# Three quarters of the MLP's second product as block multiplications with seven products each, on one Trainium2 core

## The chip, the core and the metric

The kernel runs on one core of one Trainium2 chip. The metric is the device time of one execution in microseconds (us). Before the change it is 3232.65 us, the median of 3 runs (3231.36 to 3234.63).

## What is computed

The reference is one inference step of a decoder with two trunk layers, run for 1024 prompt positions and 8 sample positions together (T = 1032 columns), model width D = 1024. Each layer is a mixer, a cross-attention into a memory, and an MLP with squared ReLU and hidden width 4096. Cut to what matters here:

```python
for l in range(DEPTH):                                  # DEPTH = 2
    x = x + mix                                         # pooling + RWKV-7 in layer 0, gated MLP in layer 1
    x = x + cross_attn(rmsnorm(x, norm_xa_g[l]), ...)
    x = x + sq_relu_mlp(rmsnorm(x, norm_ffn_g[l]), w_ff_up[l], w_ff_down[l])

def sq_relu_mlp(h, w_up, w_down):
    return jnp.square(jax.nn.relu(h @ w_up)) @ w_down
```

The change is in the product with `w_ff_down`: 4096 rows (32 K tiles of 128) by 1024 columns, times the hidden activations (4096 by 1032).

## The kernel before

All activations lie transposed, in tiles of 128 partitions by T columns. X is 8 such tiles, hidden is 32. A factor in fp32 is split into two fp32r parts: ScalarE copies the high part (line 194), and VectorE or GpSimd subtracts it from the source to get the low part (line 195). Three matmuls (high by high, high by low, low by high) then stand for one product. SBUF for tiles of T columns is a list of 42 slots that `get` takes from the front and `put` gives back at the end (lines 142 to 150); a load into a slot waits for the slot's last reader.

The MLP is `ffn` (line 1619).

**The first product** (line 1664) already goes through `strassen` (line 405). K and T are halved and the output rows go in pairs, so that a block of two output tiles by two halves of T takes seven half-size products instead of eight. A product is 24 matmuls of 258 columns: two quarters of T, four K tiles, three matmuls each (lines 426 to 428). For the left factors, `Left.make` (line 381) loads two weight units per pair (tag wraw, two buffers), forms up to four sums on VectorE and splits seven half-units into the tags whi and wlo (two buffers each). The right factors (`ops`, seven times four tiles) are made once. `collect` (line 437) takes the results out of PSUM and adds them up: ScalarE copies the first three, VectorE adds the rest, GpSimd adds twice (lines 452 and 456). `store` (line 1626) scales, squares and writes each half of a hidden tile to DRAM (hdn).

**The second product** (lines 1669 to 1704) is done in K blocks of 4, 8, 8, 8 and 4 tiles. The hidden tiles of a block are loaded from hdn and split (`hidden`, line 1633) while the block before it is computed. A block of 4 runs through `down` (line 1585), in the last layer the last one through `last` (line 1602). A block of 8 loops over the 8 output tiles: one weight unit, three groups of columns (384, 384, 264), 24 matmuls each, and VectorE adds the group from PSUM to X (line 1697). So a block of 8 has 192 matmuls each of three column groups, 576 in all.

A scheduler of the tile layer sets the order on each queue when the kernel is built; each engine and SyncE's DMA queue then work strictly in that order.

Of the kernel before, what the change touches and what calls it, by code (L numbers as in the profile page):

```python
# [74 lines left out]
SKIP = (0, 2)  # L75
STAY = 4
# [49 lines left out]
def hybrid_step(ctx: ExitStack, tc: tile.TileContext, I, O):  # L126
# [243 lines left out]
    class Left:  # L370


        def __init__(self, units):
            self.u, self.n, self.done = units, 0, deque()
# [6 lines left out]
        def make(self):  # L381
# [16 lines left out]
            split((a1, t, b1, t, a2, a2, b2)[j], w[:, 0:512], w[:, 512:1024])  # L398
# [970 lines left out]
    hdn = dr.tile([2, NFF, 128, T], F32, name="hdn")  # L1369

# [231 lines left out]
    def last(units, hid, nx):  # L1602

        wus = [(get(F32R), get(F32R)) for _ in units]
        for src, (hi, lo) in zip(units, wus):
            raw = sb.tile([128, 1024], F32, tag="wraw", bufs=2, name=nm("wr"))
            sy.dma_start(out=raw, in_=src)
            split(raw, hi[:, 0:1024], lo[:, 0:1024])
        nx.lag = LAG
        for g, (g0, g1) in enumerate(GR):  # L1610
            for m in range(KT):
                wh, wl = [t[:, (m % 2) * 512 : (m % 2) * 512 + 512] for t in wus[m // 2]]
# [6 lines left out]
    def ffn(l, nx, nname, then=None):  # L1619
# [23 lines left out]

        cur, w0, n = [], [], NFF // 2 * 7

        def fill(i):
# [8 lines left out]
            if j == 0:  # L1655
                raw = get()
                w0.extend(hpair())
                sy.dma_start(out=raw[:, 0:1024], in_=I[f"wd{l}"][0])
                split(raw[:, 0:1024], w0[0][:, 0:1024], w0[1][:, 0:1024])
                put(raw)  # L1660
# [3 lines left out]
        strassen(Left([I[f"wu{l}"][m] for m in range(NFF)]), nx.ops, lambda *a: collect(st, *a, store), fill=fill)  # L1664
# [4 lines left out]
        sizes = [4, 8, 8, 8, 4]  # L1669
        starts = [sum(sizes[:i]) for i in range(len(sizes))]  # L1670
        n2 = None
        for i, (k0, n) in enumerate(zip(starts, sizes)):
            nxt = []
            ahead = deque(range(starts[i + 1], starts[i + 1] + sizes[i + 1]) if i + 1 < len(sizes) else ())
            units = I[f"wd{l}"][k0 : k0 + n]
            if i == len(sizes) - 1:
                n2 = Next(None) if then else NextS(nname, xd[2])
                n2.lag = max(n2.lag, LAG)
                if then:
                    n2.then = lambda g: then(n2, g)  # L1680
                    last(units, cur, n2)
                    continue

            def more_hidden(k=1):
                for _ in range(min(k, len(ahead))):
                    nxt.append(hidden(ahead.popleft()))
# [354 lines left out]
```

## Time and profile before

| | |
|---|---|
| median of 3 runs | 3232.65 us |
| the profiled execution | 3233.54 us, span 3231.8 us |
| TensorE busy | 3138.2 us (97%), 22974 matmuls |
| VectorE, ScalarE, GpSimd busy | 59%, 36%, 20% |
| granted TensorE clock, mean | 0.986 |
| DMA | 416.07 MB, mean 129 GB/s |
| second product, blocks of 8 K tiles, layer 0 | about 1336 to 1609 us of the span |
| the same, layer 1 | about 2899 to 3170 us |

Matmul records overlap, so the length of one is not what it costs: the distance from one start to the next is. The same holds, less so, for VectorE, whose records overlap by 0.08 us where it has no wait. A row of the timeline gives start, length, engine, line, operation, output from input, shape and count, and in brackets the idle time before it with what ended it. The page names tiles without their numbers.

### The profile page before, as it was taken

What the parts mean: (1) busy time and instruction counts of PE and PEld (TensorE: products, weight loads), DVE (VectorE), ACT (ScalarE), POOL (GpSimd) and SP (SyncE); (2) the same over time, 40 slices, a digit from 0 to 9 for tenths busy, and PEclk for the clock granted to TensorE, in tenths of its full rate; (3) what the DMA queues carried; (4) which work ended last, traced back from release to release, by engine and by line L of the source; (5) the groups of instructions that cost most, each with busy time, mean ns of one, the idle gap of its engine ahead of it and who ended that gap; (6) DMA issues with size and microseconds to landing.
All of it is one profiled execution on the core that took longest, in us unless ns stands there. A gap on an engine that the chain in (4) does not pass through costs nothing.

```text
span 3231.8 us, 56258 instructions
## 1 busy us (share of the span) xinstructions
PE 3138.2 (97%) x22974; PEld 3015.0 (93%) x22974; DVE 1907.2 (59%) x3271; ACT 1162.7 (36%) x2218; POOL 651.2 (20%) x582
## 2 busy tenths in 40 slices
PE   8999799999999999999999999999999999999998
PEld 7988678898799999999999989899989999999998
DVE  4688644645457666532287897846445766662334
ACT  5223243434354444311163444224334544430111
POOL 5223334320031111000043351213002211100003
PEclk9999899999999999999999999999999999999999
DMA  3345677633423335432123354524342233461221
GB/s 120 119 144 188 125 244 230 223 108 116 159 92 102 106 118 181 159 104 67 48 91 126 112 200 154 171 72 138 118 165 99 87 106 112 131 233 54 91 72 66
DMA packets 188177, 416.07 MB, mean 129 GB/s; under 512 B 44301, under 2 KB 69261, under 8 KB 187918
## 3 DMA queue, kind: packets, MB, share of 16 engines
q1 hardware_dynamic: 168078, 392.01, 36.4%
q10 hardware_dynamic: 19840, 20.45, 2.3%
q8 instruction: 181, 2.97, 0.4%
q14 instruction: 78, 0.64, 0.1%
HBM read 297.23 MB, written 115.16 MB: 128 GB/s over the span
## 4 chain that ended last, share of the span: by engine, by line
PE 78%; DVE 10%; DMA 6%; ACT 2%; issue 2%; POOL 1%; SPq 0%; ACTq 0%; DVEq 0%; POOLq 0%
PE ps L225 15%; PE ps L226 15%; PE ps L227 15%; PE ps L428 8%; PE ps L426 8%; PE ps L427 8%; DVE s L195 1%; DVE wp L195 1%; DVE s L480 1%; PE ps L1469 1%; DMA wr<-in_w_in_c 1%; PE ps L1497 1%; PE ps L1825 1%; DMA wr<-in_wv 1%; DVE s L198 0%
## 5 line engine op out<-in xcount | busy, mean ns | idle before, releaser
L225 PE MATMUL ps<-s,wh 128*128 128x384 f32 (+2 forms) x3242 | 1046.4, 323 | 15.3 <-ACT wh L194 14.1
L227 PE MATMUL ps<-s,wl 128*128 128x384 f32 (+2 forms) x3242 | 1037.1, 320 | 2.7 <-DVE wl L195 2.7
L226 PE MATMUL ps<-s,wh 128*128 128x384 f32 (+2 forms) x3242 | 1038.2, 320 | 0.0
L426 PE MATMUL ps<-s,wp 128*128 128x258 f32 x2688 | 766.1, 285 | 3.6 <-DVE s L480 2.1
L428 PE MATMUL ps<-s,wp 128*128 128x258 f32 x2688 | 764.9, 285 | 4.2 <-DVE wp L195 4.2
L427 PE MATMUL ps<-s,wp 128*128 128x258 f32 x2688 | 762.6, 284 | 0.0
L225 PEld LDWEIGHTS ps<-s,wh 128*128 128x128 f32 x3242 | 612.5, 189 | 26.4 <-ACT wh L194 15.0
L227 PEld LDWEIGHTS ps<-s,wl 128*128 128x128 f32 x3242 | 611.5, 189 | 9.2 <-DVE wl L195 4.1
L226 PEld LDWEIGHTS ps<-s,wh 128*128 128x128 f32 x3242 | 612.3, 189 | 7.5 <-issue 6.0
L428 PEld LDWEIGHTS ps<-s,wp 128*128 128x128 f32 x2688 | 512.0, 191 | 6.5 <-DVE wp L195 6.2
L426 PEld LDWEIGHTS ps<-s,wp 128*128 128x128 f32 x2688 | 511.9, 190 | 6.0 <-issue 3.1
L427 PEld LDWEIGHTS ps<-s,wp 128*128 128x128 f32 x2688 | 512.9, 191 | 0.0
L265 POOL TENSOR_TENSOR s<-s,m 128x384 f32<-128x384 f32 (+1 forms) x147 | 164.0, 1124 | 1295.7 <-ACT m L264 1294.7
L194 ACT CAST wh<-wr 128x1024 fp32r<-128x1024 f32 x162 | 169.8, 1049 | 655.2 <-PE ps L226 598.3
L195 DVE TENSOR_TENSOR wp<-wr,wp 128x512 fp32r<-128x512 f32 x240 | 226.6, 944 | 177.6 <-ACT wp L194 176.5
L1697 DVE TENSOR_TENSOR s<-ps,s 128x384 f32<-128x384 f32 x144 | 74.3, 516 | 338.7 <-PE ps L227 338.7
L195 DVE TENSOR_TENSOR wl<-wr,wh 128x1024 fp32r<-128x1024 f32 x149 | 185.4, 1245 | 79.9 <-ACT wh L194 77.4
L194 ACT CAST wp<-wr 128x512 fp32r<-128x512 f32 x240 | 149.2, 622 | 148.5 <-PE ps L428 68.2
L195 DVE TENSOR_TENSOR s<-s,s 128x516 fp32r<-128x516 f32 (+4 forms) x168 | 158.0, 954 | 48.5 <-ACT s L194 47.6
L194 ACT CAST s<-s 128x516 fp32r<-128x516 f32 (+4 forms) x168 | 129.0, 788 | 87.0 <-DMA s<-hdn 43.2
L452 POOL TENSOR_TENSOR s<-s,s 128x516 f32<-128x516 f32 x40 | 59.2, 1480 | 490.7 <-ACT s L451 459.0
L1630 ACT ACTIVATE s<-s 128x516 f32<-128x516 f32 x128 | 81.3, 635 | 152.2 <-DVE s L478 152.2
(322 smaller groups left out, 4003.5 us busy)
## 6 DMA issues: line engine op xcount, KB each, us to landing
hdn<-s SPq DMA_DIRECT2D x128, 258.0 KB, 2.0
s<-hdn SPq DMA_DIRECT2D x64, 516.0 KB, 5.7
wr<-in_wu SPq DMA_DIRECT2D x64, 512.0 KB, 3.7
wr<-in_wd SPq DMA_DIRECT2D x62, 512.0 KB, 3.6
s<-in_kc SPq DMA_DIRECT2D x64, 256.0 KB, 3.9
s<-in_vc SPq DMA_DIRECT2D x64, 256.0 KB, 3.5
wr<-in_w_in_c SPq DMA_DIRECT2D x32, 512.0 KB, 3.7
xd<-s SPq DMA_DIRECT2D x24, 516.0 KB, 2.7
```

Of the source, the lines that this page charges most:

```text
L194: se.copy(out=hi, in_=src)
L195: (eng or ve).tensor_tensor(out=lo, in0=src, in1=f(hi), op=ALU.subtract)
L225: te.matmul(out, wh, xh, start=i == 0, stop=False)
L226: te.matmul(out, wh, xl, start=False, stop=False)
L227: te.matmul(out, wl, xh, start=False, stop=i == n - 1)
L265: po.tensor_tensor(out=self.acc[:, g0:g1], in0=self.acc[:, g0:g1], in1=sq, op=ALU.add)
L426: te.matmul(out, wh, xh, start=j < 4 and k == 0, stop=False, skip_group_check=j >= 4)
L427: te.matmul(out, wh, xl, start=False, stop=False, skip_group_check=j >= 4)
L428: te.matmul(out, wl, xh, start=False, stop=k == 3, skip_group_check=j >= 4)
L452: (eng or po).tensor_tensor(out=v, in0=v, in1=c12, op=ALU.add)
L1630: se.activation(out=t, in_=t, func=AF.Square)
L1697: ve.tensor_tensor(out=X[m][:, g0:g1], in0=ps, in1=X[m][:, g0:g1], op=ALU.add)
```

## The change

The 24 K tiles between the first 4 and the last 4 go through `strassen` too, in three blocks of 8. The first 4 and the last 4 stay as they were (`plain`, or `last` in the last layer), with the loading of their units moved about.

- Right factors. In the first product, when a pair of hidden tiles is finished, `pair_done` makes the four sums of halves that the seven products need with four subtractions on GpSimd, and writes them to DRAM (hts, two tiles of T columns). This is done for 12 of the 16 pairs. In the second product, `right` loads one factor of 516 columns from hdn or hts and splits it; for each fourth one the low part is made on GpSimd. A block takes 28 of them. Those of the first block are made during the first `plain`, 6 ahead of each weight unit and 4 after it; those of the next block during the last seven products of a block (`refill`), each four after the product whose factors they replace.
- Left factors. `Left` gets a set of products, (2, 5), whose low part is made on GpSimd. The host orders each block's K tiles as evens and odds.
- Results. `add_x` adds them to X, GpSimd for one of the four halves of a pair.

```diff
+HEAD = 4
     class Left:
-        def __init__(self, units):
-            self.u, self.n, self.done = units, 0, deque()
+        def __init__(self, units, pool=()):
+            self.u, self.n, self.done, self.pool = units, 0, deque(), pool
...
-            split((a1, t, b1, t, a2, a2, b2)[j], w[:, 0:512], w[:, 512:1024])
+            split((a1, t, b1, t, a2, a2, b2)[j], w[:, 0:512], w[:, 512:1024], eng=po if j in self.pool else None)
...
+        def pair_done(mp, b, a):
+            if 2 * mp >= HEAD and 2 * mp < NFF - HEAD:
+                ta, tb = get(), get()
+                for o, x, y in ((ta[:, 0:HT], b[:, HT:T], b[:, 0:HT]), (ta[:, HT:T], a[:, HT:T], b[:, HT:T]),
+                                (tb[:, 0:HT], a[:, HT:T], ta[:, 0:HT]), (tb[:, HT:T], a[:, 0:HT], tb[:, 0:HT])):
+                    po.tensor_tensor(out=o, in0=x, in1=y, op=ALU.subtract)
+                for i, t in enumerate((ta, tb)):
+                    sy.dma_start(out=hts[l, mp, i], in_=t)
+                put(ta, tb)
+            put(a, b)
+
+        def right(j, k, p):
+            src = (hd[2 * p][:, 0:HT], hts[l, p, 0][:, 0:HT], hts[l, p, 0][:, HT:T], hts[l, p, 1][:, 0:HT],
+                   hd[2 * p + 1][:, 0:HT], hd[2 * p + 1][:, HT:T], hts[l, p, 1][:, HT:T])[j]
+            t = get(F32R)
+            sy.dma_start(out=f(t[:, HT:T]), in_=src)
+            split(f(t[:, HT:T]), t[:, 0:HT], t[:, HT:T], eng=po if k == 3 else None)
+            return t
...
+        def early():
+            for j, k in order[:6]:
+                ops[j].append(right(j, k, p0 + k))
+            del order[:6]
+
+        plain(0, cur, w0, None, early)
+        for j, k in order:
+            ops[j].append(right(j, k, p0 + k))
...
+        def add_x(m, h, t, src):
+            x = X[m][:, h * HT : (h + 1) * HT]
+            for q, (o, p) in enumerate(halves(x, src) if src else ((x, t),)):
+                (po if m % 2 and h else ve).tensor_tensor(out=o, in0=p, in1=o, op=ALU.add)
+
+        for blk in range(3):
+            nxt = [[] for _ in range(7)]
+            def refill(i):
+                j = i - 21
+                if j < 0:
+                    return
+                put(*ops[j])
+                if blk < 2:
+                    for k in range(4):
+                        nxt[j].append(right(j, k, p0 + 4 * blk + 4 + k))
+                elif j in (1, 2):
+                    cur.extend(hidden(NFF - HEAD + 2 * j - 2 + k) for k in range(2))
+                elif j == 0 or then and j > 2 and j < 6:
+                    w0.append(held_unit(wd[NFF - HEAD + len(w0)]))
+            strassen(Left([wd[HEAD + 8 * blk + m] for m in range(KT)], (2, 5)), ops, lambda *a: collect(st, *a, add_x), fill=refill)
+            ops = nxt
```

In the program that is built, the order of the instructions moves at three places. The changed program's lines stand 1 to 2 lower in the helpers than before: line 195 (the low part of a split) is now 196, line 378 (a unit for `Left`) is 379.

SyncE's DMA queue where a block of 8 in layer 0 ends and the next begins (hdn and hts are the hidden tiles and their sums in DRAM, in_wd the weights, wr the buffer of a weight unit, s a slot). Before, the units of both blocks stand in one run, with the hidden tiles of the block after that behind them:

```order
L204 DMA wr_14310<-in_wd 128x1024
L204 DMA wr_14399<-in_wd 128x1024
L204 DMA wr_14488<-in_wd 128x1024
L204 DMA wr_14577<-in_wd 128x1024
L1635 DMA s_14484<-hdn 128x1032
L1635 DMA s_14573<-hdn 128x1032
```

In the changed program, at the end of the first of the three blocks:

```order
L1658 DMA s_14820<-hdn 128x516
L1658 DMA s_14824<-hdn 128x516
L1658 DMA s_14855<-hts 128x516
L1658 DMA s_14859<-hts 128x516
L1658 DMA s_14863<-hts 128x516
L1658 DMA s_14867<-hts 128x516
L379 DMA wr_14871<-in_wd 128x1024
L379 DMA wr_14873<-in_wd 128x1024
```

The first two weight units of the next block (wr_14871, wr_14873) now stand behind all 28 right factors of that block, the last of which is s_14867.

VectorE at the same place. Before, the last group of the block is added to X (s_13161 is X's last tile), then come the low parts for the block, and the first group of the next block (s_13115 is X's first tile):

```order
L1697 TENSOR_TENSOR s_13161<-ps_14342,s_13161 128x384
L1697 TENSOR_TENSOR s_13161<-ps_14368,s_13161 128x264
L195 TENSOR_TENSOR wl_14490<-wr_14488,wh_14489 128x1024
L195 TENSOR_TENSOR s_14484<-s_14484,s_14483 128x1032
L195 TENSOR_TENSOR s_14573<-s_14573,s_14572 128x1032
L1697 TENSOR_TENSOR s_13115<-ps_14405,s_13115 128x384
```

In the changed program (s_14812 to s_14863 are right factors, ps is PSUM, wp_14876 the first left factor of the next block, L467 and L1715 the last results of the block on their way to X):

```order
L196 TENSOR_TENSOR s_14812<-s_14812 128x516
L196 TENSOR_TENSOR s_14816<-s_14816 128x516
L196 TENSOR_TENSOR s_14820<-s_14820 128x516
L467 TENSOR_TENSOR s_14574<-ps_14645,s_14574 128x258
L467 TENSOR_TENSOR s_14574<-ps_14646,s_14574 128x258
L196 TENSOR_TENSOR s_14855<-s_14855 128x516
L1715 TENSOR_TENSOR s_13258<-s_14574,s_13258 128x516
L196 TENSOR_TENSOR s_14859<-s_14859 128x516
L196 TENSOR_TENSOR s_14863<-s_14863 128x516
L196 TENSOR_TENSOR wp_14876<-wr_14871,wp_14876 128x512
L391 TENSOR_TENSOR m_14875<-wr_14873 128x512
```

The low part of the next block's first left factor stands behind VectorE's share of the right factors, 21 rows of line 196. Between wp_14642, the left factor of the fifth of the block's last seven products, and wp_14876 there are 31 rows: the last 19 right factors, one sum of weights, the left factor wp_14739 of the block's last product, two adds from SBUF to X, and 8 rows that read PSUM.

GpSimd during the first product. Before, two adds per pair of output tiles:

```order
L452 TENSOR_TENSOR s_9466<-s_9466,s_9467 128x516
L456 TENSOR_TENSOR s_9466<-s_9466 128x516
L452 TENSOR_TENSOR s_9763<-s_9763,s_9764 128x516
L456 TENSOR_TENSOR s_9763<-s_9763 128x516
L452 TENSOR_TENSOR s_9998<-s_9998,s_9999 128x516
```

In the changed program, for 12 of the 16 pairs:

```order
L453 TENSOR_TENSOR s_9999<-s_9999,s_10000 128x516
L457 TENSOR_TENSOR s_9999<-s_9999 128x516
L1647 TENSOR_TENSOR s_10204<-s_10000 128x516
L1647 TENSOR_TENSOR s_10204<-s_9999,s_10000 128x516
L1647 TENSOR_TENSOR s_10205<-s_9999,s_10204 128x516
L1647 TENSOR_TENSOR s_10205<-s_9999,s_10205 128x516
```

The four subtractions of `pair_done` stand behind the two adds. At the end of a block of the second product GpSimd has, between its left factor wp_14691 (of the last product but one) and the start of the next block, that factor, six right factors and three adds, ten rows of 512 or 516 columns.

More of the change, by code (lines that the diff above doesn't have):

```diff
@@ L1655, in fill @@
             if j == 0:
[L1656 to L1660, printed above, removed]
+                w0.append(held_unit(wd[0]))
             if j in (1, 2):
                 load_x(range(4 * j - 4, 4 * j))
-        strassen(Left([I[f"wu{l}"][m] for m in range(NFF)]), nx.ops, lambda *a: collect(st, *a, store), fill=fill)
+        strassen(Left([I[f"wu{l}"][m] for m in range(NFF)]), nx.ops, lambda *a: collect(st, *a, store, pair_done), fill=fill)
@@ L1665, in ffn @@
         put(row)
         wide[0] = True
[L1669 to L1686, printed above, removed]
-            if n == 4:
-                units = [units[u] for u in range(4)]
-                if i == 0:
-                    units[0] = tuple(w0)
-                down(units, cur, n2, lambda: more_hidden(2))
-                if i == 0:
-                    put(*w0)
-            else:
-                def ev(m, g, g0, g1, ps):
-                    ve.tensor_tensor(out=X[m][:, g0:g1], in0=ps, in1=X[m][:, g0:g1], op=ALU.add)
-                for m in range(KT):
-                    more_hidden()
-                    linear([units[m]], lambda _: [(m, range(8))], cur, ev)
-                for x, y in cur:
-                    put(x, y)
-            cur = nxt
@@ new lines, in plain @@
+        def plain(k0, hid, w, nx, between=None):
+            units = w + [wd[k0 + u] for u in range(len(w), 4)]
+            down(units, hid, nx, between)
+            for a, b in w:
+                put(a, b)
+        ops = [[] for _ in range(7)]
+        order = [(j, k) for j in range(7) for k in range(4)]
+        p0 = HEAD // 2
+        def early():
[3 more added lines that the diff above has]
+        plain(0, cur, w0, None, early)
@@ L1705, in ffn @@
+        n2 = Next(None) if then else NextS(nname, xd[2])
+        n2.lag = max(n2.lag, LAG)
+        if then:
+            n2.then = lambda g: then(n2, g)
+            last(w0, cur, n2)
+        else:
+            plain(NFF - HEAD, cur, w0, n2)
         return n2
@@ L1977, in layout @@
         wd = A["w_ff_down"][l]
-        out[f"wd{l}"] = np.concatenate([_blocks(wd[:512])] + [_units(wd[k : k + 1024]) for k in range(512, 3584, 1024)]
+        out[f"wd{l}"] = np.concatenate([_blocks(wd[:512])] + [_units(_evens(wd[k : k + 1024])) for k in range(512, 3584, 1024)]
                                        + [_blocks(wd[3584:])])
```

18 lines of the change are left out of this document (12 added, 6 removed).

## Prediction

> **What bounds the kernel now.** I read the page's first part and the chain that ended last, then the stages of the MLP by windows and waits, then single rows for durations.
>
> ```profile
> PE 3138.2 (97%) x22974; PEld 3015.0 (93%) x22974; DVE 1907.2 (59%) x3271; ACT 1162.7 (36%) x2218; POOL 651.2 (20%) x582
> PE 78%; DVE 10%; DMA 6%; ACT 2%; issue 2%; POOL 1%; SPq 0%; ACTq 0%; DVEq 0%; POOLq 0%
> ```
>
> TensorE is busy 97% of the span and holds 78% of the chain, so time goes with the number and length of its matmuls wherever the other engines keep up. In the first product, which already runs as block multiplications, they do: the window below has no idle TensorE, with VectorE at 67% and GpSimd at 13%, and the waits of TensorE between 953 and 1289 us come to 0.8 us (the last two rows: total, times, longest).
>
> ```profile
> core 0: us, PE busy (x) PEld busy (x) DVE busy (x) ACT busy (x) POOL busy (x), PEclk, DMA share, GB/s
> 1000.00:1100.00 100.00, 100.00 (x835) 100.00 (x834) 66.99 (x109) 43.15 (x85) 12.84 (x10) 1.00 0.32 106
> PE ps L428 <- DVE wp L195: 0.6, 2, 0.4
> PE ps L426 <- ACT wp L194: 0.2, 1, 0.2
> ```
>
> The three blocks of the second product that change have only TensorE as their bound too; their rows of VectorE's adds give their length (72 adds of a layer, first and last start):
>
> ```profile
> L1697 DVE TENSOR_TENSOR s<-ps,s x72: 432/557/559, 1340.7 to 1608.6; 128x384 f32<-128x384 f32 x48, 128x264 f32<-128x264 f32 x24
> L1697 DVE TENSOR_TENSOR s<-ps,s x72: 432/557/559, 2902.9 to 3170.3; 128x384 f32<-128x384 f32 x48, 128x264 f32<-128x264 f32 x24
> ```
>
> **Part 1: TensorE's work.** The distance between starts is a matmul's cost. Rows of the timeline, 96 matmuls of 258 columns apart, and 20 of 384 apart:
>
> ```profile
> 1149.80 0.28 PE L428 MATMUL ps<-s,wp 128*128 128x258 f32 x1
> ...
> 1161.33 0.29 PE L428 MATMUL ps<-s,wp 128*128 128x258 f32 x1
> ```
>
> ```profile
> 1302.37 0.34 PE L225 MATMUL ps<-s,wh 128*128 128x384 f32 x1
> ...
> 1305.88 0.34 PE L227 MATMUL ps<-s,wl 128*128 128x384 f32 x1
> ```
>
> That is 11.53/96 = 0.1201 us and 3.51/20 = 0.1755 us, each about 0.46 us per 1000 columns, so the cost goes with the columns. The adds span 267.9 and 267.4 us; with the first group's 24 matmuls (24 x 0.1755 = 4.2) the three blocks take 272.1 and 271.6 us, 543.7 together. After, a block is 28 products of 24 matmuls: 672 x 0.1201 = 80.7 us, six blocks 484.2. Saved: **59.5 us**. In the Trainium skill's TensorE: Matmul & The Clock Gate, Back-to-back issue gap, sustained matmuls stand 81 ns apart at 128 columns and 131 ns at 512; a straight line between these would be 98 ns at 258, 99 at 264 and 114 at 384 (an estimate from that page), by which a block would be 672 x 98 ns = 65.9 us after and 192 x (2 x 114 + 99) ns = 62.8 us before, so the change would lose 3 us a block. The rows here disagree (176 ns at 384), and the sum goes by them.
>
> **Part 2: where one block ends and the next begins.** This happens twice a layer, four times in all. Nothing of the next block's left factors is made ahead: its first one stands on VectorE behind the 21 right factors that VectorE splits, and its weight unit stands on SyncE's queue behind all 28 loads. TensorE stops until that low part is done. Count from the start of the last seven products, which take 7 x 24 x 0.1201 = 20.2 us. VectorE's rows in that queue cost what lies between their starts where nothing waits, and what they cost beside GpSimd is seen in a stretch where both engines have a full queue:
>
> ```profile
> 1100.79 1.72 DVE L195 TENSOR_TENSOR wp<-wr,wp 128x512 fp32r<-128x512 f32 x1 [0.27 <-ACT wp L194]
> ...
> 1104.31 0.68 DVE L392 TENSOR_TENSOR wr<-wr,wr 128x512 f32<-128x512 f32 x1
> 1104.91 0.68 DVE L195 TENSOR_TENSOR wp<-m,wp 128x512 fp32r<-128x512 f32 x1
> 1105.51 0.41 DVE L462 TENSOR_TENSOR s<-ps,s 128x258 f32<-128x258 f32 x1
> 1105.85 0.68 DVE L394 TENSOR_TENSOR m<-m,wr 128x512 f32<-128x512 f32 x1
> ```
>
> ```profile
> 1100.67 1.30 POOL L456 TENSOR_TENSOR s<-s 128x516 f32<-128x516 f32 x1 [1.68 <-DVE s L455]
> 1617.56 1.02 POOL L265 TENSOR_TENSOR s<-s,m 128x384 f32<-128x384 f32 x1 [334.15 <-ACT m L264]
> 1873.93 5.19 POOL L1763 TENSOR_TENSOR s<-s,m 128x384 f32<-128x384 f32 x4 [0.24 <-ACT m L1762]
> ```
>
> ```profile
> 1874.50 1.16 DVE L392 TENSOR_TENSOR wr<-wr,wr 128x512 f32<-128x512 f32 x1
> 1875.59 1.50 DVE L480 TENSOR_TENSOR s<-s,s 128x516 f32<-128x516 f32 x1
> 1877.01 1.23 DVE L195 TENSOR_TENSOR wp<-m,wp 128x512 fp32r<-128x512 f32 x1
> 1878.16 0.42 DVE L466 TENSOR_TENSOR s<-ps,s 128x258 f32<-128x258 f32 x1
> 1878.50 1.16 DVE L195 TENSOR_TENSOR wp<-wr,wp 128x512 fp32r<-128x512 f32 x1
> ```
>
> A row with both inputs in SBUF costs 0.60 us, one that reads PSUM 0.34. Beside a GpSimd row the first kind is held up (1.72 instead of 0.68 at 1100.79, while GpSimd ran from 1100.67 to 1101.97); the second is not (0.42 at 1878.16). In the full queue the four held rows take 5.05 instead of 4 x 0.68 = 2.72 us, 0.58 for each of GpSimd's four rows. Those are 384 wide, 1.02 us undisturbed; ours are 516 wide, 1.30 undisturbed, 0.28 longer, so I take 0.86 us for each of them, between 0.58 and the 1.04 of the lone case.
>
> The chain starts with the third right factor, the first whose slot is not long free: the slot's last reader is the previous pair's last add, after product 20 (2 x 0.34 + 0.60 = 1.3 us), then a load, then ScalarE's copy. For a load of 258 KB and the copy the nearest rows are
>
> ```profile
> m<-ud SPq DMA_DIRECT2D x32, 256.0 KB, 3.3
> L194 ACT CAST s<-s 128x516 fp32r<-128x516 f32 x13 | 7.6, 625 | 2.2 <-DVE s L365 2.2
> ```
>
> so it starts at 1.3 + 3.3 + 0.6 = 5.2 us. From there VectorE has 23 rows of 0.60, 8 of 0.34 and the next block's first left factor, 0.60: 17.1 us. GpSimd's ten rows in that stretch add 10 x 0.86 = 8.6. The left factor is ready at 5.2 + 17.1 + 8.6 = 30.9 us, and TensorE had ended at 20.2: it stands **10.7 us**. The products inside the seven don't wait: the last one's left factor has 8 VectorE rows and 4 or 5 GpSimd rows ahead of it, ready at about 5.2 + 4.8 + 4.3 = 14.3 us, and is wanted at 6/7 x 20.2 = 17.3.
>
> After such a pause TensorE comes back at half clock. In this pause of 3.6 us and in the one behind it (PEclk is the first number after the five busy times):
>
> ```profile
> 172.00:174.00 2.00, 0.00 (x0) 0.00 (x0) 2.00 (x2) 1.14 (x2) 1.97 (x1) 1.00 0.99 382
> 174.00:176.00 2.00, 0.40 (x3) 0.43 (x4) 2.00 (x4) 0.03 (x1) 0.50 (x2) 0.95 0.71 274
> 176.00:178.00 2.00, 2.00 (x10) 2.00 (x9) 2.00 (x2) 1.17 (x2) 2.00 (x2) 0.50 0.02 6
> 178.00:180.00 2.00, 2.00 (x9) 2.00 (x9) 1.94 (x3) 0.00 (x0) 0.18 (x1) 0.69 0.88 283
> ...
> ```
>
> ```profile
> 580.00:582.00 2.00, 2.00 (x15) 1.55 (x14) 1.07 (x4) 0.03 (x1) 1.92 (x2) 0.50 0.68 272
> 582.00:584.00 2.00, 2.00 (x8) 1.68 (x9) 1.97 (x3) 1.91 (x4) 2.00 (x3) 0.50 0.03 8
> 584.00:586.00 2.00, 2.00 (x14) 1.71 (x14) 2.00 (x3) 0.16 (x1) 1.47 (x2) 0.65 0.38 131
> ```
>
> the first loses 2 x (0.05 + 0.50 + 0.31) = 1.7 us and the second 2 x (0.50 + 0.50 + 0.35) = 2.7; I take 2.2. A block's end thus costs 10.7 + 2.2 = 12.9 us, four of them **51.6 us**.
>
> **Part 3: the rest.** In the ordinary products VectorE has per pair 11 rows of 0.60, 8 of 0.34 and 5 GpSimd rows beside it, 6.6 + 2.7 + 4.3 = 13.6 of 20.2 us, and a left factor is made three products ahead; this costs nothing as long as that holds. In the first product GpSimd gets four rows more per pair: with its two adds 6 x 1.30 = 7.8 of 20.2 us, and VectorE's 67% grow by 4 x 0.86 = 3.4 us to some 84%. Each is under the pair's time; the stores of hts that SyncE waits for are due before the next pair's weight units, whose buffers come free only two products on. I put 0.5 us a layer, between nothing and 4. The 28 right factors of the first block lie in the first `plain` (288 matmuls, 192 of 384 columns and 96 of 264: 192 x 0.1755 + 96 x 0.12 = 45 us): VectorE has there 21 x 0.60 plus the 24 adds and three units that it had before, GpSimd 7 rows. Entry to the first block and exit from the third I put at 1 us each a layer, between 0 and 3: the right factors stand on the queue ahead of the second weight unit, and what is hidden there is hidden by the first unit's 11 us of matmuls. The rest of the layout is the host's. Together **5 us**.
>
> **The sum.** Against its own execution of 3233.54 us: 3233.54 - 59.5 + 51.6 + 5 = **3230.6 us**, 2.9 us less. That execution is 0.9 us above the median of 3232.65, which is inside the runs' spread. A measurement of this kernel can tell about 0.2% from no change, 6.5 us, so this is no difference.
>
> **Rivals.** *The pause is set by the loads, not by VectorE* (faster). If GpSimd's rows fall mostly beside PSUM rows and gaps, VectorE alone would be done at 5.2 + 17.1 = 22.3 us and the loads are the end. They ask for 4 x 0.264 MB per 2.89 us, 366 GB/s, and the fastest stretch of the stage gives
>
> ```profile
> 1300.00:1308.00 8.00, 7.67 (x51) 7.34 (x50) 8.00 (x11) 5.73 (x6) 0.00 (x0) 1.00 0.93 363
> ```
>
> so they keep pace: the last four are issued at 17.3 us, when the last product starts, take 2.9, the two weight units 2.9 more, with 2.6 of fixed time (3.3 us to landing less 0.264 MB at 363 GB/s), then 0.6 of ScalarE and 0.7 of VectorE: 27.0, a pause of 6.8, with the clock 9.0, four times 36. That gives 3233.54 - 59.5 + 36 + 5 = **3215 us**. For it speaks that no single GpSimd row is on the path by itself; against it that GpSimd's rights come with the same loads as VectorE's.
>
> *VectorE and GpSimd take turns at the block ends, row by row* (slower). If each of the ten GpSimd rows holds VectorE for its whole 1.30 us, the left factor is ready at 5.2 + 17.1 + 13.0 = 35.3: a pause of 15.1, with the clock 17.3, four times 69, and 3233.54 - 59.5 + 69 + 5 = **3248 us**. For it speak the row of 1.72 us, against it the full queue of 1873.93, where 0.58 of a row's 1.02 us fell on VectorE. The change loses from a cost of (59.5 - 5)/4 = 13.6 us per block end on. The Trainium skill's SBUF — State Buffer, Who interferes with whom, states this rule: a VectorE instruction with two SBUF inputs and a GpSimd instruction that reads SBUF exclude each other, and the loser is blocked for the whole instruction. By that rule the change ends here, at 3248 us; the trace agrees that such rows are held and PSUM rows not, and shows less than the whole row as the delay in a full queue.
>
> *The matmuls don't get cheaper, or the first product stalls behind GpSimd.* If the 12 pairs a layer each cost 1 us on the path, 24 us more: 3255 us. Against it: the slack of part 3. That the matmuls get no cheaper, as by the line that part 1 sets beside its rows, those rows rule out: nothing of the 0.04 is for it.
>
> **How the numbers follow.** My case 0.50, the pause by loads 0.32, turns 0.14, the last 0.04. Within my case the start, the delay per row (0.58 to 1.04) and the clock move a block end by 2.5 us either way, the sum by 10: faster 0.35, same 0.45, slower 0.20. Faster 0.5 x 0.35 + 0.32 = 0.50; same 0.22; slower 0.5 x 0.20 + 0.14 + 0.04 = 0.28. The range goes from the rival by loads with no loss for the clock and nothing for the rest (3233.5 - 59.5 + 4 x 6.8 = 3201) to a little above the case of turns: 3201 to 3254.
>
> **What would show it.** In the changed kernel's trace: matmuls of 258 columns 0.120 us apart in the three blocks; at each block's end one pause of about 11 us, ended by VectorE's low part of the next block's first left factor (line 196, wp), with VectorE busy throughout and ScalarE long done, then some 4 us at half clock. A pause of about 7 us ended by ScalarE or a load of in_wd is the first rival; one of 15 with GpSimd and VectorE both full the second. Waits of TensorE spread over the blocks, or over the first product, would make my reading wrong; so would no pause at all, which needs the left factor to be ready before the right ones.

## The result, and the profile after

| | before | after |
|---|---|---|
| median (runs) | 3233.30 us (4) | 3265.68 us (4) |
| lowest to highest | 3231.36 to 3234.63 | 3263.68 to 3271.79 |
| the profiled execution, span | 3233.54, 3231.8 | 3267.47, 3265.4 |
| granted TensorE clock, mean | 0.986 | 0.975 |

The ratio is 1.0104, 95% interval 1.0086 to 1.0121: the change makes the kernel 1% slower. The forecast was 3230.6 us and a range that ended at 3254.

The first part of the page and the chain that ended last, after the change:

```profile
PE 3100.5 (95%) x23550; PEld 2970.8 (91%) x23550; DVE 2194.6 (67%) x3613; ACT 1305.4 (40%) x2602; POOL 1040.4 (32%) x840
PE 68%; DVE 15%; DMA 8%; issue 4%; POOL 3%; ACT 3%; SPq 0%; ACTq 0%; DVEq 0%; POOLq 0%
```

TensorE's busy time fell by 37.7 us, while its share of the chain fell from 78 to 68% and VectorE's rose from 10 to 15%: work was taken off TensorE, and more than that came back as time in which it waits.

Where it waits is read by stages. The matmuls of the first product, those of the line that begins each group of three, before and then after, one row per layer (first and last start):

```profile
L426 PE MATMUL ps<-s,wp x896: 277/283/387, 961.4 to 1289.6; 128*128 128x258 f32 x180
L426 PE MATMUL ps<-s,wp x896: 277/282/389, 2523.1 to 2849.4; 128*128 128x258 f32 x180
```

```profile
L427 PE MATMUL ps<-s,wp x896: 277/283/420, 963.3 to 1303.1; 128*128 128x258 f32 x180
L427 PE MATMUL ps<-s,wp x896: 276/282/420, 2544.5 to 2881.4; 128*128 128x258 f32 x180
```

It went from 328.2 to 339.8 us in layer 0 and from 326.3 to 336.9 in layer 1. The forecast had put half a microsecond on each. The same line in the three blocks of each layer, after:

```profile
L427 PE MATMUL ps<-s,wp x672: 277/283/584, 1356.0 to 1627.9; 128*128 128x258 f32 x168
L427 PE MATMUL ps<-s,wp x672: 275/282/584, 2933.2 to 3204.0; 128*128 128x258 f32 x168
```

With the last group of three (0.3 us) they take 272.2 and 271.1 us. Before, by the starts of their matmuls (1336.00 to 1608.39 and 2898.03 to 3170.14), it was 272.4 and 272.1: the pauses between the blocks eat nearly all that the cheaper blocks save. From the first product's end to the first block, the first `plain` stage, it is 1356.0 - 1303.5 = 52.5 us, against 46.0 before; in layer 1 51.4 against 48.3. The last `plain` of layer 0 and `last` of layer 1 moved by under 1 us. What is left, some 3 us, lies in stages that the change doesn't touch.

The end of the first block in layer 0, from TensorE's timeline; the brackets give the idle time before a row and what ended it:

```profile
1436.65 0.28 PE L429 MATMUL ps<-s,wp 128*128 128x258 f32 x1
1442.70 0.58 PE L427 MATMUL ps<-s,wp 128*128 128x258 f32 x1 [5.77 <-ACT wp L195]
1443.08 0.42 PE L428 MATMUL ps<-s,wp 128*128 128x258 f32 x1
1443.30 0.42 PE L427 MATMUL ps<-s,wp 128*128 128x258 f32 x1
1450.52 0.58 PE L429 MATMUL ps<-s,wp 128*128 128x258 f32 x1 [6.81 <-DVE wp L196]
```

and the windows behind the second wait, PEclk being the first number after the busy times:

```profile
1450.00:1452.00 2.00, 1.48 (x7) 1.48 (x8) 1.95 (x4) 0.75 (x2) 0.00 (x0) 0.50 0.00 0
1452.00:1454.00 2.00, 2.00 (x11) 2.00 (x11) 1.19 (x2) 1.36 (x3) 1.43 (x1) 0.50 0.04 8
1454.00:1456.00 2.00, 2.00 (x16) 2.00 (x16) 0.86 (x1) 0.88 (x3) 0.36 (x1) 0.85 0.00 0
```

TensorE's last product ends its issue at 1436.77; a high part made by ScalarE lets three matmuls through at 1442.70; the low part made by VectorE at 1449.79 lets it go on at 1450.52, for 4 us at half clock. It is the pause of the forecast, ended by the row that it named, and longer; that a high part made by ScalarE ends a first part of it was not forecast.

The other loss is at the first product's end. The waits of TensorE in the first product of layer 0, after (total, times, longest), and the rows where they stand:

```profile
PE ps L429 <- DVE wp L196: 3.6, 4, 1.7
PE ps L427 <- ACT wp L195: 3.1, 2, 2.0
PE ps L427 <- DVE s L479: 0.7, 1, 0.7
```

```profile
1249.69 0.39 PE L427 MATMUL ps<-s,wp 128*128 128x258 f32 x1 [1.02 <-ACT wp L195]
1251.91 0.39 PE L429 MATMUL ps<-s,wp 128*128 128x258 f32 x1 [1.71 <-DVE wp L196]
1276.19 0.39 PE L427 MATMUL ps<-s,wp 128*128 128x258 f32 x1 [2.05 <-ACT wp L195]
1277.93 0.58 PE L429 MATMUL ps<-s,wp 128*128 128x258 f32 x1 [1.24 <-DVE wp L196]
```

From 1030, where the subtractions of `pair_done` begin, to 1249, where the last pair but one begins, TensorE doesn't wait at all. What begins just there is `hidden`: the four hidden tiles of the first `plain` are loaded and cast. ScalarE's timeline and SyncE's queue (SPq) at the first of the two places:

```profile
1243.05 0.62 ACT L195 CAST wp<-wr 128x512 fp32r<-128x512 f32 x1 [2.94 <-DVE wr L397]
1243.58 0.37 ACT L452 COPY s<-ps 128x258 f32<-128x258 f32 x1
1247.79 1.05 ACT L195 CAST s<-s 128x1032 fp32r<-128x1032 f32 x1 [3.84 <-DMA s<-hdn]
1248.75 0.37 ACT L452 COPY s<-ps 128x258 f32<-128x258 f32 x1
1249.02 0.62 ACT L195 CAST wp<-wr 128x512 fp32r<-128x512 f32 x1
```

```profile
1242.45 0.32 SPq L1649 DMA_DIRECT2D hts<-s  x1
1242.86 1.50 SPq L1632 DMA_DIRECT2D s<-hdn  x2
1244.43 0.40 SPq L379 DMA_DIRECT2D wr<-in_wu  x1
```

The load of the hidden tile (s<-hdn) stands on the queue behind a store of differences (hts<-s), which waits for GpSimd. ScalarE runs its instructions in the program's order: it stands 3.84 us before the cast of that tile, and the cast of a left factor (wp) for which TensorE waits stands behind it. In the first product of layer 0 SyncE's waits before these stores come to 61.6 us in 24 times, the longest 2.8:

```profile
SPq L1649 <- POOL s L1647: 61.6, 24, 2.8
```

### The profile page after: what moved, and what is told of

Its sections match the earlier page's. It is cut to its first block, busy times and chain, and to the rows that moved or that the text cites. A ratio compares the mean times of both kernels' runs of the same rounds, so it can differ in the third digit from the quotient of the medians.

```text
span 3265.4 us, 59432 instructions
## 1 busy us (share of the span) xinstructions
PE 3100.5 (95%) x23550; PEld 2970.8 (91%) x23550; DVE 2194.6 (67%) x3613; ACT 1305.4 (40%) x2602; POOL 1040.4 (32%) x840
## 4 chain that ended last, share of the span: by engine, by line
PE 68%; DVE 15%; DMA 8%; issue 4%; POOL 3%; ACT 3%; SPq 0%; ACTq 0%; DVEq 0%; POOLq 0%
PE ps L429 10%; PE ps L428 10%; PE ps L427 10%; PE ps L226 10%; PE ps L227 9%; PE ps L228 9%; DVE s L196 3%; DVE wp L196 2%; DMA wr<-in_w_in_c 2%; DVE s L481 1%; DMA s<-hdn 1%; POOL s L1647 1%; PE ps L1471 1%; DMA wr<-in_wu 1%; PE ps L1499 1%
## 5 line engine op out<-in xcount | busy, mean ns | idle before, releaser
L429 PE MATMUL ps<-s,wp 128*128 128x258 f32 x4032 | 1152.6, 286 | 37.8 <-DVE wp L196 37.7
L427 PE MATMUL ps<-s,wp 128*128 128x258 f32 x4032 | 1154.0, 286 | 33.5 <-ACT wp L195 28.6
L428 PE MATMUL ps<-s,wp 128*128 128x258 f32 x4032 | 1150.1, 285 | 0.0
L429 PEld LDWEIGHTS ps<-s,wp 128*128 128x128 f32 x4032 | 773.2, 192 | 43.0 <-DVE wp L196 42.7
L427 PEld LDWEIGHTS ps<-s,wp 128*128 128x128 f32 x4032 | 772.5, 192 | 38.5 <-ACT wp L195 31.6
L428 PEld LDWEIGHTS ps<-s,wp 128*128 128x128 f32 x4032 | 774.5, 192 | 0.0
L226 PE MATMUL ps<-s,wh 128*128 128x384 f32 (+2 forms) x2066 | 673.7, 327 | 25.4 <-ACT wh L195 23.2
L227 PE MATMUL ps<-s,wh 128*128 128x384 f32 (+2 forms) x2066 | 665.7, 323 | 0.2
L228 PE MATMUL ps<-s,wl 128*128 128x384 f32 (+2 forms) x2066 | 661.0, 321 | 1.3 <-DVE wl L196 1.3
L196 DVE TENSOR_TENSOR wp<-wr,wp 128x512 fp32r<-128x512 f32 x312 | 319.2, 1024 | 249.5 <-ACT wp L195 248.6
L226 PEld LDWEIGHTS ps<-s,wh 128*128 128x128 f32 x2066 | 393.7, 191 | 37.1 <-ACT wh L195 24.3
L227 PEld LDWEIGHTS ps<-s,wh 128*128 128x128 f32 x2066 | 393.4, 190 | 8.1 <-issue 6.0
L228 PEld LDWEIGHTS ps<-s,wl 128*128 128x128 f32 x2066 | 391.9, 190 | 7.0 <-issue 4.1
L195 ACT CAST wp<-wr 128x512 fp32r<-128x512 f32 x360 | 223.5, 622 | 287.2 <-DVE wr L397 62.8
L196 DVE TENSOR_TENSOR wl<-wr,wh 128x1024 fp32r<-128x1024 f32 x100 | 125.8, 1258 | 58.5 <-ACT wh L195 58.2
L453 POOL TENSOR_TENSOR s<-s,s 128x516 f32<-128x516 f32 x64 | 89.9, 1405 | 214.2 <-ACT s L452 214.2
L195 ACT CAST wp<-m 128x512 fp32r<-128x512 f32 x144 | 89.2, 619 | 172.4 <-DVE m L391 110.1
L196 POOL TENSOR_TENSOR wp<-wr,wp 128x512 fp32r<-128x512 f32 x48 | 66.1, 1378 | 280.4 <-ACT wp L195 280.4
## 6 DMA issues: line engine op xcount, KB each, us to landing
hdn<-s SPq DMA_DIRECT2D x128, 258.0 KB, 2.0
s<-hts SPq DMA_DIRECT2D x96, 258.0 KB, 5.0
s<-hdn SPq DMA_DIRECT2D x72, 258.0 KB, 4.9
s<-in_kc SPq DMA_DIRECT2D x64, 256.0 KB, 4.0
s<-in_vc SPq DMA_DIRECT2D x64, 256.0 KB, 2.9
```

The source lines that it names most:

```text
L195: se.copy(out=hi, in_=src)
L196: (eng or ve).tensor_tensor(out=lo, in0=src, in1=f(hi), op=ALU.subtract)
L226: te.matmul(out, wh, xh, start=i == 0, stop=False)
L227: te.matmul(out, wh, xl, start=False, stop=False)
L228: te.matmul(out, wl, xh, start=False, stop=i == n - 1)
L427: te.matmul(out, wh, xh, start=j < 4 and k == 0, stop=False, skip_group_check=j >= 4)
```

## The experiments

Each was timed beside runs of the kernel before on the same chip, whose median was 3233.06 us (19 runs) for e1 to e4, 3235.35 (19) for e5 to e8 and 3232.93 (8) for e9 to e12. Lengths of stages are given for layers 0 and 1 and run to the first matmul of the next stage, 0.4 us more than the rows above show; by that measure the first product takes 328.6 and 326.6 us before, 340.2 and 337.3 after. My theory was that queue order makes both losses: left factors behind right factors at the blocks' ends, and hidden tiles behind stores in the first product. The rivals were VectorE held up by GpSimd, too much work on VectorE, and bytes.

**e1: the next block's left factors first.**

```diff
+        lefts = [Left([wd[HEAD + 8 * b + m] for m in range(KT)], (2, 5)) for b in range(3)]
...
                 put(*ops[j])
+                if blk < 2 and j >= 4:
+                    lefts[blk + 1].make()
                 if blk < 2:
...
-            strassen(Left([wd[HEAD + 8 * blk + m] for m in range(KT)], (2, 5)), ops, lambda *a: collect(st, *a, add_x), fill=refill)
+            strassen(lefts[blk], ops, lambda *a: collect(st, *a, add_x), fill=refill)
```

> The changed kernel, but the first three left factors of the next block are made inside the last three products of a block, ahead of the right factors of those products, instead of behind all 28. Theory: the pause at a block's end (13.6 us at 1436.7 us, with the half clock about 15) is there because the first left factor stands last on VectorE's, ScalarE's and SyncE's queues. It then is ready about when TensorE ends, and what is left is some 4 us before the fourth product, whose left factor still stands behind the last right factors: about 6.5 us per end instead of 15, 4 x 8.5 = 34 us less than the changed kernel, about 3232 us. Rival: VectorE and GpSimd simply have too much work there, and the pause only moves a few products on: less than 8 us gained in all, 3258 to 3266 us.

Measured: 3236.39 us (10 runs), ratio 1.0014 (1.0001 to 1.0027), 29.3 us less than the changed kernel, where 34 were expected. The blocks take 259.2 and 256.0 us, 13 and 15 less. The waits of TensorE in layer 0's blocks, after and then e1:

```profile
PE ps L429 <- DVE wp L196: 13.2, 2, 6.8
PE ps L427 <- ACT wp L195: 11.5, 2, 5.8
```

```profile
PE ps L427 <- DVE s L467: 7.7, 2, 3.8
PE ps L429 <- DVE wp L196: 3.3, 4, 1.5
```

Eleven microseconds are left there of 25. Close to half of the blocks' loss was the place of the left factors. What TensorE now waits for (L467) is an add in the results of the last products, also on VectorE.

**e2: the hidden tiles one pair earlier.**

```diff
-            if -7 <= j < -3:
-                cur.append(hidden(j + 7))
+            if -14 <= j < -10:
+                cur.append(hidden(j + 14))
```

> The changed kernel, but the four hidden tiles for the first plain block are loaded one pair (seven products) earlier in the first product. Theory: the stall near the end of the first product (1274 us, 3.5 us, and half clock after it) comes from the fourth of these loads standing on SyncE's queue behind a store of hts that waits for GpSimd, with ScalarE's copy of it ahead of the copy that TensorE needs. The two first products then lose at least 6 us each of their 11, 13 to 20 us in all: 3246 to 3253 us. Rival: GpSimd's four subtractions per pair hold VectorE up, wherever the loads stand: within 4 us of the changed kernel's 3265.7.

Measured: 3264.01 us (4 runs), ratio 1.0094 (1.0066 to 1.0122). My expectation fell, and by its number the rival, that GpSimd's subtractions hold VectorE up wherever the loads stand, held; e5 below decides against it. The first products are 337.7 and 334.5 us, and the waits moved with the loads: they begin at 1227.77, one pair earlier than in the changed kernel. SyncE's queue in e2 says why:

```profile
1218.82 0.32 SPq L1649 DMA_DIRECT2D hts<-s  x1
1219.24 1.21 SPq L1632 DMA_DIRECT2D s<-hdn  x2
```

Twelve pairs store differences, so one pair earlier the loads stand behind the stores of another pair.

**e3: no subtractions, no stores.** The pair's tiles are released at once, and all right factors are loaded from hdn, so four of the seven are other data (the diff shows the first of the two changes).

```diff
-            if 2 * mp >= HEAD and 2 * mp < NFF - HEAD:
+            if False:
```

> The changed kernel without GpSimd's four subtractions and the stores of hts; every right factor is loaded from the hidden tiles instead, so four of the seven products of a block use wrong factors. Loads, splits and matmuls of the second product are as many as before. Both theories of the first product: it takes 328 us again instead of 340 and 337, so 20 to 24 us less, 3242 to 3246 us. If less than 10 us go, the first product's loss has another cause (the later loads of the right factors, or the first weight units). The gap to the kernel with the earlier loads of hidden tiles is what the subtractions themselves cost.

Measured: 3234.47 us (10 runs), ratio 1.0007 (0.9994 to 1.0021), 8 us better than the low end of what I expected. The first products are at 327.9 and 327.5 us, as before the change, and the first `plain` at 48.8 and 50.3.

**e4: all right factors on VectorE.**

```diff
-            split(f(t[:, HT:T]), t[:, 0:HT], t[:, HT:T], eng=po if k == 3 else None)
+            split(f(t[:, HT:T]), t[:, 0:HT], t[:, HT:T], eng=None)
```

> The changed kernel, but all right factors get their low part on VectorE, none on GpSimd: at a block's end VectorE has 6 or 7 rows of 0.60 us more and GpSimd 6 rows fewer. If the two take turns and each GpSimd row holds VectorE for its whole 1.30 us: -7.8 + 4.2 = 3.6 us less per end, 14 us less in all, 3251 us. If a GpSimd row costs VectorE 0.86 us as in the prediction: -5.2 + 4.2, 4 us less in all, 3262 us. If GpSimd's rows cost VectorE nothing: 4 us more per end, 17 us more, 3282 us.

Measured: 3255.04 us (4 runs), ratio 1.0067 (1.0041 to 1.0092). The total lies between two expectations, but only 4.6 of its 10.6 us lie in the blocks (268.8 and 270.0 us), 1.15 for each block end. The first products, where this edit changes nothing, are 6 us shorter; in the experiments that leave them as they are they vary by 3 us each. The blocks vary less (271.6 to 272.0 us in e2 and e5, which leave them alone), so they answer: VectorE took seven rows of 0.60 more at each end and was still 1.15 us earlier, so the seven GpSimd rows had cost it (4.2 + 1.15)/7 = 0.76 us each. That is the mean over a whole refill. My 0.86 was near; the whole row, 1.30, is too much.

**e5: the hidden tiles before the first stores.**

```diff
-            if -7 <= j < -3:
-                cur.append(hidden(j + 7))
+            if 14 <= i < 18:
+                cur.append(hidden(i - 14))
```

> The four hidden tiles of the first plain stage are loaded and cast at pairs 2 of the first product (products 14 to 17), before any pair has subtractions or stores behind which they could stand; all else is as in the changed kernel. Theory A (the first product's 11.6 and 10.7 us are lost at its end, because the loads of the hidden tiles stand on SP behind stores that wait for GpSimd, and ScalarE's casts, in order, stand behind those loads): both first products come back to 329 to 331 us, and the time to 3245 to 3250. Theory B (GpSimd's subtractions slow VectorE's rows all through the last pairs, wherever the loads are): within 5 us of 3265.7. Theory C (any load in that stretch stands behind a store, the left factors' too): between the two, 3253 to 3261, with the stalls now on the casts of the left factors.

Measured: 3239.90 us (10 runs), ratio 1.0020 (1.0010 to 1.0031), 25.8 us less than the changed kernel and 5 below the low end of theory A. The first product of e5 in layer 0, and all of TensorE's waits in it:

```profile
L427 PE MATMUL ps<-s,wp x896: 277/283/386, 963.4 to 1291.5; 128*128 128x258 f32 x180
PE ps L429 <- DVE wp L196: 0.6, 2, 0.4
```

It takes 328.1 us, the 328.2 of before, with every subtraction and store in place; layer 1 has 326.9. VectorE's rows beside GpSimd are still long there (1.67 us at 1236.58 for a row of 0.68), and cost nothing. The first `plain` fell to 49.4 in both layers, which theory A had not counted.

**e6: subtractions without stores; e7: stores without subtractions.** In both, four of the seven right factors are other data (e6 loads them from hdn, which its diff here does not show).

```diff
-                for i, t in enumerate((ta, tb)):
-                    sy.dma_start(out=hts[l, mp, i], in_=t)
```

> GpSimd makes its four subtractions in each pair, but their results are not stored, and four of the seven right factors are loaded from the hidden tiles instead of from the differences (so those products are computed from other data). Leaves out 24 stores a layer. Theory A (stores that wait for GpSimd hold SP's queue): the first products come back to 329 to 331 us, 3242 to 3248. Theory B (the subtractions slow VectorE beside them): within 6 us of 3265.7.

```diff
-                ta, tb = get(), get()
-                for o, x, y in ((ta[:, 0:HT], b[:, HT:T], b[:, 0:HT]), (ta[:, HT:T], a[:, HT:T], b[:, HT:T]),
-                                (tb[:, 0:HT], a[:, HT:T], ta[:, 0:HT]), (tb[:, HT:T], a[:, 0:HT], tb[:, 0:HT])):
-                    po.tensor_tensor(out=o, in0=x, in1=y, op=ALU.subtract)
-                for i, t in enumerate((ta, tb)):
+                for i, t in enumerate((b, a)):
                     sy.dma_start(out=hts[l, mp, i], in_=t)
-                put(ta, tb)
```

> The two tiles of each pair are stored in place of the differences, with no subtraction at all (four of the seven right factors are therefore other data); the same bytes are stored and the same loads made. Theory A and theory B: without a wait for GpSimd and without rows beside VectorE, the first products are at 328 to 331 us, 3242 to 3248. Rival C (the bytes or the number of stores are what costs): 338 to 340 us each, within 5 us of 3265.7.

Measured: e6 3256.77 us (4 runs), ratio 1.0072 (1.0050 to 1.0093), first products 334.0 and 333.2; e7 3238.69 us (10 runs), ratio 1.0018 (1.0003 to 1.0033), first products 328.1 and 327.4. The stores and their bytes alone cost nothing. The subtractions alone cost about half: ScalarE's waits in e6 at the first product's end are

```profile
ACT s L195 <- DMA s<-hdn: 19.2, 7, 5.5
```

so its casts still stand before late hidden tiles. e6 fell between its two expectations: the stall needs the hidden tiles at that place and GpSimd's subtractions, and the stores on the queue make it about twice as long. SyncE's waits in e6's first product of layer 0 show what makes the loads late with no stores ahead of them:

```profile
SPq L1632 <- POOL s L1647: 10.6, 3, 4.4
```

Three of the four loads (L1632) themselves wait for a subtraction on GpSimd (L1647), which a load into a slot does when GpSimd used that slot last. So in both kernels SyncE stands behind GpSimd, in the changed one before a store, here before the load.

**e8: no right factors for the second and third block.** All three blocks use those of the first.

```diff
+                if blk < 2:
+                    nxt[j] = ops[j]
+                    return
                 put(*ops[j])
-                if blk < 2:
-                    for k in range(4):
-                        nxt[j].append(right(j, k, p0 + 4 * blk + 4 + k))
-                elif j in (1, 2):
+                if j in (1, 2):
```

> No right factors are made for the second and third block: all three blocks use those of the first (so two blocks compute from other data, and 56 loads and casts a layer are left out). Theory (the left factors of the next block stand on SP, ScalarE and VectorE behind the right factors, 14.7 us at each of four ends): the pauses go, the blocks take 241 to 246 us a layer, and the time is 3265.7 - 59 = 3207, between 3203 and 3214. Rival (what holds TensorE at a block's end is the evictions into X or the left factors' own chain from load to cast): 3250 or above.

Measured: 3205.78 us (4 runs), ratio 0.9912 (0.9890 to 0.9933), 59.9 us less than the changed kernel. Its blocks:

```profile
L427 PE MATMUL ps<-s,wp x672: 278/283/289, 1353.3 to 1595.2; 128*128 128x258 f32 x168
L427 PE MATMUL ps<-s,wp x672: 277/282/289, 2900.7 to 3141.8; 128*128 128x258 f32 x168
```

They take 242.2 and 241.4 us, with no wait of TensorE in those of layer 0. So the four block ends of the changed kernel cost 30.0 and 29.7 us a layer, 14.9 each, and the refill, with its loads, casts and low parts, is all of that.

**e9: e1 and e5 together.**

> Both corrections of order at once: the first three left factors of a block are made inside the last three products of the block before, ahead of the right factors, and the hidden tiles of the first plain stage are loaded at products 14 to 17 of the first product. Theory (two separate losses, one at the blocks' ends, one at the first product's end): the two gains add, 29.3 and 25.8 us off 3265.7, which is 3210.6, between 3207 and 3216. Rival (both gains come from one shared excess of work on VectorE, which is only shifted): less than half of the smaller gain is added, 3224 or above.

Measured: 3210.73 us (5 runs), ratio 0.9941 (0.9914 to 0.9967), which is 55.0 us less than the changed kernel where the two gains give 55.1. First products 328.5 and 326.7, blocks 257.5 and 258.0. The two corrections of order take away two separate losses, and with both the change is worth 0.6%.

**e10 to e12: what is left at the block ends.** e10 adds e4 to e9. e11 adds to e9 four right factors made early:

```diff
                 j = i - 21
+                if blk < 2 and -6 <= j < -2:
+                    nxt[0].append(right(0, j + 6, p0 + 4 * blk + 10 + j))
...
-                    for k in range(4):
-                        nxt[j].append(right(j, k, p0 + 4 * blk + 4 + k))
+                    for k in range(4 if j < 6 else 0):
+                        nxt[j + 1].append(right(j + 1, k, p0 + 4 * blk + 4 + k))
```

e12 has both, and the second weight unit of the first `plain` loaded in the first product:

```diff
-            if j == 0:
-                w0.append(held_unit(wd[0]))
+            if j in (0, 3):
+                w0.append(held_unit(wd[len(w0)]))
...
-            for j, k in order[:6]:
+            for j, k in order[:5]:
...
-            del order[:6]
+            del order[:5]
```

> As e9_both, and all low parts of right factors on VectorE, none on GpSimd. What is left of the wait at a block's end there is 5.2 us at each of four ends in the kernel with the left factors ahead. Theory (GpSimd's rows block VectorE while VectorE is the bound there): 6 to 12 us faster than e9_both, 3199 to 3205. Rival (VectorE has now seven more rows of 0.68 us in each refill, and GpSimd's were in its shadow): 0 to 8 us slower than e9_both.

> As e9_both, and the four right factors of the next block's first product are made at products 15 to 18 of a block, in four free tiles, so that each of the last seven products makes the right factors of the product after its own number. Theory (what is left at a block's end is the rate at which VectorE, ScalarE and the queue make 28 factors within 20.2 us): four factors of about 0.7 to 1 us less at each of four ends, 10 to 16 us faster than e9_both, 3195 to 3201. Rival (the latency of the first product's own factors and the evictions that precede it are what is left): within 4 us of e9_both.

> All of the corrections together: left factors ahead, hidden tiles first, no rows of right factors on GpSimd, four right factors early, and the first plain stage's second weight unit loaded at the end of the first product rather than behind the right factors. Theory: the blocks come near the 241 to 242 us that they take without any refill (243 to 250), the first plain stage to 46 to 48 us, and the time to 3185 to 3198. Rival (VectorE's share of the work is the bound, whatever the order): not below e11_both_spare by more than 4 us.

Measured: e10 3207.54 us, ratio 0.9918 (0.9897 to 0.9938); e11 3214.12, 0.9936 (0.9921 to 0.9951); e12 3206.69, 0.9911 (0.9896 to 0.9926), 4 runs each. None is told apart from e9 by its interval. e10 lies 3.2 us below e9, where neither of its expectations had put it. e11's theory fell and its rival held by the number (3.4 us above e9). In e12 both fell: the blocks were to take 243 to 250 us, and the time is 7.4 below e11's where the rival allowed 4. By stages that gain is the first `plain` (8.3 us less than in e11, both layers together), and the blocks stay at 255.6 to 260.5 us, 13 to 18 above e8's, whatever the order. VectorE at the end of the first block in e1 points to why (busy times of TensorE, weight loads, VectorE, ScalarE, GpSimd):

```profile
1420.00:1440.00 20.00, 14.70 (x119) 14.07 (x117) 19.96 (x24) 11.79 (x23) 13.05 (x9) 0.97 0.70 252
```

It has no idle time there while the right factors are made, so moving them moves the wait. In the blocks of layer 0 nearly all of TensorE's waits in e9 to e11 end at a row of VectorE (10.5, 8.9 and 12.5 us), in e12 6.7 of 12.5. That VectorE's work is the bound is argued from this and not shown: no run took work off VectorE alone, and e8 left out loads and casts as well. One part of e12 does what it should: its first `plain` takes 45.1 and 45.5 us, against 47.5 and 49.6 in e9. e12 and e10 are the fastest versions that compute everything, 0.9 and 0.8% below the kernel before.

## Why the prediction was wrong, by its steps

Against the profiled executions, 3267.47 is 36.9 us above the forecast.

*Part 1 was right.* A matmul of 258 columns costs 0.12 us in the blocks too: e8's blocks take 483.6 us together, 484.2 were forecast. The straight line through the spacings of the Trainium skill's TensorE: Matmul & The Clock Gate, Back-to-back issue gap, would have made it 3 x 65.9 = 198 us a layer (the prediction's estimate from that page); 242 was measured.

*Part 2 had the mechanism right and the size too small.* The block end costs 14.9 us instead of 12.9, four times 2.0 = 8 us. Its terms can be read in the trace of after, at the first of the four ends, where the stop is the longest (13.7 us from the last issue to 1450.52; 12.7 to 13.4 at the others). The last seven products start 20.2 us before 1436.77, at 1416.6. VectorE's first rows for the right factors:

```profile
1422.35 0.83 DVE L196 TENSOR_TENSOR wp<-wr,wp 128x512 fp32r<-128x512 f32 x1 [2.46 <-ACT wp L195]
1423.46 0.70 DVE L196 TENSOR_TENSOR s<-s 128x516 fp32r<-128x516 f32 x1 [0.28 <-ACT s L195]
...
1449.79 0.68 DVE L196 TENSOR_TENSOR wp<-wr,wp 128x512 fp32r<-128x512 f32 x1
```

The row at 1423.46 comes 6.9 us after the start instead of 5.2: VectorE had stood 2.46 us for a left factor whose cast on ScalarE was behind one that waited for a load. To the end of the left factor's low part at 1450.47 it takes 27.0 us, against 17.1 + 8.6 = 25.7. Ready at 33.9 us instead of 30.9, then, and 1.7 + 1.3 is the difference. The rows in that stretch are those of the forecast, so GpSimd's ten cost 27.0 - 17.1 = 9.9 us there, 0.99 each instead of 0.86. There are two pauses rather than one, since a high part comes first. The clock was sized well: TensorE's waits in the blocks of layer 0 come to 24.7 us, 12.4 for each end, which leaves 2.6 of 15.0, and the windows shown lose 2 x (0.50 + 0.50 + 0.15) = 2.3, where 2.2 was forecast. What was too small is the stop itself. The rival in which GpSimd's rows hold VectorE wholly had 17.3 for a block end, so the measurement lies about halfway between. GpSimd's rows there:

```profile
1438.23 6.78 POOL L196 TENSOR_TENSOR s<-s 128x516 fp32r<-128x516 f32 x4
```

They take 1.70 us each instead of 1.30, beside VectorE rows of 1.3 to 1.8 us instead of 0.68: both engines are slowed where they meet. The rule of the Trainium skill's SBUF — State Buffer, Who interferes with whom, that the loser is blocked for the whole instruction, fits single rows here (1.78 us for a row of 0.68); over a whole refill e4 puts 0.76 us on each GpSimd row, not 1.30. That some of GpSimd's time falls beside rows that it doesn't hold would explain this, and is not shown.

*Part 3 failed, in the term "0.5 us a layer, between nothing and 4" for the first product.* It measured 11.6 and 10.6 us, 21 us more than forecast. The step asked whether each engine's work fits into a pair's time, and it does: VectorE's share rose from 67% to 77%, under the 84% of the forecast, and GpSimd's from 13% to 38%.

```profile
1000.00:1100.00 100.00, 100.00 (x836) 100.00 (x835) 77.18 (x111) 42.81 (x85) 37.67 (x26) 1.00 0.41 145
```

What it left out is what stands behind the new stores on SyncE and, through the hidden tiles, on ScalarE. It looked only at the next pair's weight units. e5 settles it: with the hidden tiles out of that stretch the term is under 1 us a layer. The rival at 3255 us had named the first product with 24 us, close to what was lost, but by GpSimd's rows in all 12 pairs; e5 and the time from 1030 to 1249 without a wait show that this mechanism is not the one, and that its number came near is luck.

*The entry to the first block failed too, in size.* "1 us" measured 6.5 and 3.1 us, both above the 3 that it allowed. The second weight unit, which the step saw behind the right factors, was not hidden by the first unit's matmuls. TensorE's row in after:

```profile
1319.90 0.69 PE L226 MATMUL ps<-s,wh 128*128 128x384 f32 x1 [4.94 <-ACT wh L195]
```

In e5, which leaves that unit in its place, the same wait is 2.5 us, so about half of it had come with the late hidden tiles. e12, where the unit comes earlier, takes it away. Exit from the third block was under 1 us, as forecast or less.

The sum: 8 us from the block ends, less 1 that the blocks' matmuls saved beyond the forecast, 21 from the first product, 8 from the entry, 3 from stages that the change leaves alone, 2 less at the exits: 37 of the 36.9.

## What to carry to other kernels

A cost that fits an engine's share of a stage can still stop TensorE, when an instruction that waits stands ahead of an urgent one in an in-order queue: for every wait that a change adds (here a store, or a load into a slot, behind GpSimd), list what stands behind it on that queue, and then what stands behind that on the next engine, up to the stage's end and its neighbour's loads. Operands that the next stage needs belong ahead of the bulk work and not at its end. When reordering stops helping, as here with 13 to 18 us a layer left, see whether the engine that makes the operands is full over that stretch; less work for it is then what is left to try.

## What the runs showed that I had not expected

Of GpSimd's four subtractions for a pair, all of 516 columns, the first takes 1.30 us and the other three 1.75 (rows of the changed kernel's first product, layer 0, minimum, median and maximum in ns; L453 is the first of the two adds):

```profile
L1647 POOL TENSOR_TENSOR s<-s,s x36: 1623/1750/1783, 1030.8 to 1266.2; 128x516 f32<-128x516 f32 x36
L1647 POOL TENSOR_TENSOR s<-s x12: 1292/1299/1306, 1029.5 to 1261.4; 128x516 f32<-128x516 f32 x12
L453 POOL TENSOR_TENSOR s<-s,s x16: 1290/1300/2107, 976.1 to 1293.9; 128x516 f32<-128x516 f32 x16
```

The first has both inputs in one tile and the others in two, but so have the adds of L453, whose median is 1.30: two tiles alone don't make a row slow. The three slow ones follow directly on another row of GpSimd, with VectorE rows that are held up beside them (1.79 us at 1031.27 for a row of 0.68); which of the two matters was not tried. And short waits cost more than their length: in the first product of layer 0 TensorE's waits come to 7.4 us and the stage is 11.6 us longer. Behind the waits of 2.05 and 1.24 us the granted clock (first number after the five busy times) stays at half for some 6 us:

```profile
1278.00:1280.00 2.00, 2.00 (x9) 2.00 (x10) 1.16 (x4) 0.00 (x0) 1.59 (x1) 0.50 0.46 123
1280.00:1282.00 2.00, 2.00 (x12) 2.00 (x11) 1.34 (x3) 1.16 (x2) 0.00 (x0) 0.50 0.36 143
1282.00:1284.00 2.00, 2.00 (x11) 2.00 (x11) 2.00 (x5) 1.15 (x2) 0.00 (x0) 0.51 0.69 264
```

That is 2 x (0.50 + 0.50 + 0.49) = 3.0 us, nearly as much again as the two waits, 3.3. Behind the waits of 1.02 and 1.71 the clock in the windows from 1252 to 1258 is 0.81, 0.50 and 0.84, another 1.7 us, and 7.4 + 3.0 + 1.7 = 12.1 accounts for the 11.6.
